# Where a mixer kernel stores its split weights, and which engine splits them before the first attention

## The chip, the cores and the metric

The kernel runs on one core of one Trainium2 chip. The metric is the device time of one execution in microseconds (us). Three executions of the kernel before gave 1756.65, 1754.84 and 1751.86 us, with a median of 1754.84 us.

## The reference, cut to what matters

One layer of a streaming encoder is computed for a prompt of 2048 rows and a sample of 32 rows, both 1024 wide and in float32.

```python
mod = c @ w_mod + b_mod                          # shift, scale, gate
h = rms_norm(x, g_pre) * (1 + scale) + shift
z = h @ w_in                                     # 1024 x 5632
a, b, z_conv, q, k, v, z_attn, g_conv, g_attn = split(z)
u = a * sigmoid(b)
y_conv = (silu(layer_norm(depthwise31(u) + dw_b)) * silu(z_conv)) @ w_conv_out
o = chunk_band_attention(q, k, v, rel_bias)      # 64-row chunks, own and 8 past chunks
y_attn = (o * silu(z_attn)) @ w_attn_out
merged = sigmoid(g_conv) * y_conv + sigmoid(g_attn) * y_attn
y = x + gate * rms_norm(merged @ w_o, g_post)
```

The new convolution rows, keys and values are returned as well.

## The kernel before, in words

The prompt is worked through in four blocks of 512 rows. Block 0 carries the 32 sample rows along, so its products have two halves of 272 columns, and the other blocks have one of 512.

Every product is done in two float32r parts. A weight W arrives in `raw` (512 KB), ScalarE copies its high part into `w`, and VectorE or GpSimd subtracts to get the low part. `w_parts` (L219) does this, and three matmuls follow for each pair of tiles. The weights come in one fixed order, the list `plan`. `weights` (L238) is called once for each of them. It splits the weight two places ahead (`w_parts(i + 2)`), loads the one four places ahead (`w_load(i + 4)`, two `raw` buffers), and stores the split one place ahead to DRAM (`w_keep(i + 1)`, 1 MB). Later uses load that 1 MB (`kept`) straight into one of three `w` buffers. `keep_at` (L207) says at which use a weight is stored. Before, the four weights of v are stored at their second use, in block 1, and all others at their first, in block 0 or, for some, behind it.

The stages of a block are these. The v projection comes first, then q and k of head pair 0. The attention follows, in units of one head and 256 query rows (or the sample), and between its parts `fill` lets the other projections run in the order of `FILL` (L54). In block 0 that order also holds eight parts `m0` to `m7` of the modulation gate (`mod_part`), four for each half, and `gate_row` finishes each half with one more matmul. After the attention come the gate projections (`C_GC`, `C_GA`, eight tiles each) with the attention's output product, then the convolution's output product, then w_o in two halves, with the a and b projections of the next block between them.

Before block 0 there is an opening stage. It computes shift and scale in four steps (`mod_load`, `mod_split`, `mod_mm`, `mod_vec`), normalises the rows, transposes them, and runs the v projection step by step.

The order on TensorE, VectorE, ScalarE and GpSimd is the order in which the program writes the instructions. It is steered by `Pace`, a clock kept by the program itself: `pace.pe` counts TensorE's time and `pace.dve` VectorE's, and `pace.start(gen, delay)` starts a side task when `pace.pe` has advanced by `delay`. The depthwise convolution's taps are such a side task (`pace.idle`). SP, which issues nearly all loads and stores, is not in that order: a planner places its DMAs, which is why `move_caches` (L594), written in block 1, is issued during block 0. ScalarE issues the stores of `w_keep`.

Which engine subtracts is decided in `w_parts`:

```python
on_v = pace.dense or pace.idle is None and pace.dve <= pace.pe + DV
(V if on_v else G).tensor_tensor(wl, raw, wh.bitcast(F32), op=OP.subtract)
```

`pace.dense` is set after the attention of block 0 and taken back after that of block 1.

Of the kernel before, what the change touches and what calls it, by code (L numbers as in the profile page):

```python
# [8 lines left out]
F32 = mybir.dt.float32  # L9
F32R = mybir.dt.float32r  # L10
I32 = mybir.dt.int32
AF = mybir.ActivationFunctionType
OP = mybir.AluOpType
# [3 lines left out]
P = 128  # L17
D = 1024
# [3 lines left out]
TB = 512  # L22
# [10 lines left out]
C_A, C_B, C_ZC, C_Q, C_K, C_V, C_ZA, C_GC, C_GA = (  # L33
    0, 512, 1024, 1536, 2048, 2560, 3072, 3584, 4608)
# [10 lines left out]
DV = -0.5  # L45
# [8 lines left out]
def FILL(b):  # L54

    part = dict(q=C_Q, k=C_K, a=C_A, b=C_B, z=C_ZA, c=C_ZC, m=C_MOD)
    order = "b0 a0 q1 m0 k1 m1 b1 m2 a1 m3 b2 q2 m4 k2 m5 a2 m6 z0 m7 b3 a3 z1 q3 k3 z2 z3 c0 c1 c2 c3" if b == 0 else \
        "q1 k1 z0 q2 k2 z1 q3 k3 z2 z3 c0 c1 c2 c3"
    return [(int(x[1]), part[x[0]]) for x in order.split()]


def dram(ap, off, dims):
    return bass.AP(tensor=ap.tensor, offset=ap.offset + off, ap=[list(d) for d in dims])
# [7 lines left out]
class Pace:  # L71


    def __init__(self):
        self.pe = 0.0
        self.dve = 0.0
        self.tasks = []
        self.idle = None
        self.lead = LEAD
        self.sinks = []  # L80
        self.dense = False

    def start(self, gen, delay=0.0):
        self.tasks.append([self.pe + delay, gen])
# [56 lines left out]
def mixer_kernel(ctx, tc, x_prompt, x_sample, c_prompt, c_sample, cache_conv, cache_k, cache_v,  # L141
# [4 lines left out]
    G = nc.gpsimd  # L146
    pace = Pace()
    V = Vec(nc, pace)

    def mm(out, lhsT, rhs, start, stop):  # L150
        n = 1
        for d in rhs.shape[1:]:
            n *= d
        pace.pe += (6 + n * 0.4063) / 1e3
        nc.tensor.matmul(out, lhsT=lhsT, rhs=rhs, start=start, stop=stop)  # L155
# [6 lines left out]
    wp = ctx.enter_context(tc.tile_pool(name="wp", bufs=2))  # L162
# [6 lines left out]
    def pp_tile(name):  # L169
        return pp.tile([P, 512], F32, tag="pp", name=name)  # L170
# [18 lines left out]
    for b in range(NB):  # L189
        plan += [w_wide("v", w_in, k, C_V) for k in range(0, KT, 2)]  # L190
        plan += [w_fill(n, c) for n, c in [(0, C_Q), (0, C_K)] + FILL(b)]
        for m in range(0, KT, 2):
            for i in range(2):
                plan += [w_cols(c + (m + i) * P) for c in (C_GC, C_GA)]
            plan.append(w_half("ao", w_attn_out, m))
        plan += [w_half("co", w_conv_out, m) for m in range(0, KT, 2)]
        plan += [w_wide("o", w_o, k, 0) for k in range(0, KT, 2)]
        if b < NB - 1:
            plan += [w_cols(c + ct * P) for ct in range(NCT) for c in (C_B, C_A)]
        plan += [w_wide("o", w_o, k, 512) for k in range(0, KT, 2)]  # L200

    uses = {}
    for i, entry in enumerate(plan):
        uses.setdefault(entry[0], []).append(i)
    keep_at = {key: at[1 if key[0] == "v" else 0] for key, at in uses.items()}  # L207
    again = {key for key, at in uses.items() if len(at) > 1}
    raws, halves, kept, used = {}, {}, {}, [0]

# [7 lines left out]
    def w_parts(i):  # L218

        if i < len(plan):  # L220
            key = plan[i][0]
            w = wp.tile([P, 2, 1024], F32R, tag="w", name="w", bufs=3)
            wh, wl = w[:, 0], w[:, 1]
            if i <= keep_at[key]:
                raw = raws.pop(i)
                act(wh, raw, AF.Copy)  # L226
                on_v = pace.dense or pace.idle is None and pace.dve <= pace.pe + DV
                (V if on_v else G).tensor_tensor(wl, raw, wh.bitcast(F32), op=OP.subtract)  # L228
            else:
                nc.sync.dma_start(w.bitcast(F32), kept[key])  # L230
            halves[i] = w
# [6 lines left out]
    def weights(key):  # L238
        i = used[0]
        assert plan[i][0] == key, (i, plan[i][0], key)  # L240
        used[0] += 1
        w_parts(i + 2)
        w_load(i + 4)
        w_keep(i + 1)
        w = halves.pop(i).rearrange("p h (k c) -> p h k c", c=plan[i][1])
        return w[:, 0], w[:, 1]
# [240 lines left out]
    def shape(b):  # L487
        yw = TB + (HIST + TS if b == 0 else 0)
        return TB + (TS if b == 0 else 0), yw, [(0, TB, 0)] + ([(USEP0, USEP0 + TS, TB)] if b == 0 else [])
# [74 lines left out]
    def mod_part(i):  # L564


        n, kp = i // 4, i % 4
        m4, bm, gr = aof[0:4, 3, 0:512], aof[0:2, 2, 0:512], aof[0:2, 1, 0:512]
        if kp == 0:
            nc.sync.dma_start(bm, dram(b_mod, 2 * D + n * 512, [[0, 2], [1, 512]]))  # L570
            nc.sync.dma_start(gr, dram(g_post, n * 512, [[0, 2], [1, 512]]))
        wh, wl = weights(("mod", 2 * kp, (4 + n) * 512))
        pm = pp_tile("pm")
        for kk in range(2):
            mm(pm[0:4], c4[:, 2 * kp + kk, :], wh[:, kk, :], kk == 0, False)
            mm(pm[0:4], c4[:, 2 * kp + kk, :], wl[:, kk, :], False, kk == 1)
            yield
        if kp == 0:
            act(m4, pm[0:4], AF.Copy)
        else:  # L580
            V.tensor_tensor(m4, pm[0:4], m4, op=OP.add)
        if kp == 3:
            pace.start(gate_row(n, m4, bm, gr), 1.5)

    def gate_row(n, m4, bm, gr):
        pg = pp_tile("pg")
        nc.tensor.matmul(pg[0:2], lhsT=sel, rhs=m4, start=True, stop=True)
        yield 1.5
        V.tensor_tensor(bm, pg[0:2], bm, op=OP.add)
        V.tensor_tensor(bm, bm, gr, op=OP.mult)  # L590
        nc.sync.dma_start(gp_d[:, n * 512:(n + 1) * 512], bm)
        gate_done.add(n)
        yield 0.0
# [7 lines left out]
    def spill_v(b, vcur):  # L601
        for t in range(4):
            nc.sync.dma_start(vs_d[b][:, t], vcur[:, t].bitcast(F32))
            yield 6.0
# [20 lines left out]
    with tc.tile_pool(name="init", bufs=1) as ini:  # L625
        mraw, mparts, m4 = {}, {}, {}
# [10 lines left out]
        def mod_split(c, start=0, end=4):  # L637
            mparts.setdefault(c, [])
            for i, raw in enumerate(mraw[c]):
                if i < start or i >= end:  # L640
                    continue
                wh, wl = [ini.tile([P, 4, 256], F32R, tag=n, name=n, bufs=4) for n in ("wmh", "wml")]
                act(wh, raw, AF.Copy)
                (G if i % 2 else V).tensor_tensor(wl, raw, wh.bitcast(F32), op=OP.subtract)
                mparts[c].append((wh, wl))

        pms = {}
# [42 lines left out]
        with tc.tile_pool(name="x0", bufs=5) as x0:  # L690
# [31 lines left out]
            c2 = vecs[:, 0:16].rearrange("p (a k) -> p k a", a=2)  # L722
# [7 lines left out]
            for t, (xt, m) in enumerate(xs0):  # L730
                if t % 2:
                    act(xt[0:m], xt[0:m], AF.Copy, scale=rr[0:m, t:t + 1])
                else:
                    V.tensor_scalar(xt[0:m], xt[0:m], rr[0:m, t:t + 1], None, op0=OP.mult)
            mod_mm(0, 0, 2)
            w_parts(0)
            pst = ps.tile([P, 512], F32, tag="T", name="pst", bufs=2)
            for ct in range(KT):
                transpose(pst[:, ct * TS:(ct + 1) * TS], xs0[4][0][0:TS, ct * P:(ct + 1) * P], ident[0:TS, 0:TS])
            xst = ini.tile([P, KT, TS], F32, name="xst")  # L740
            V.tensor_copy(xst, pst[:, 0:KT * TS].rearrange("p (k c) -> p k c", c=TS))
            pts = [h_turn(xs0, ct) for ct in range(2)]
            mod_split(1, 0, 2)
            mod_mm(0, 2)
            mod_vec(0)
            mod_split(1, 2, 4)
            lrow = aof.rearrange("p a c -> p (a c)")[0:H, 0:SKEW]

# [50 lines left out]


    pace.dve = pace.pe
    qls = []
    for b in range(NB):
        NT, YW, ypieces = shape(b)
# [4 lines left out]
        with tc.tile_pool(name="at", bufs=1) as at:  # L809
# [3 lines left out]
            vcur = at.tile([P, 4, H, P], F32R, name="vcur")  # L813
# [22 lines left out]
                    o = (nvs[0, 0, 512 - TS:512] if t == 4 else nvp[0, 0, t * P:(t + 1) * P])  # L836
                    nc.sync.dma_start(o.rearrange("t h d -> t (h d)"), vo[0:m, 0:512])
            if b < NB - 1:
                pace.start(spill_v(b, vcur), 30.0)

            if b < 2:

                qls.clear()
                for _ in range(2):
                    qls.append(wp.tile([P, 2, TB], F32R, tag="raw", name="ql0") if b else
                               at.tile([P, 2, NT], F32R, tag="ql", name="ql", bufs=2))
                    G.memset(qls[-1][64:128, 0].bitcast(F32), 0.0)
                    G.memset(qls[-1][0:64, 1].bitcast(F32), 0.0)


            att, cvs, ready = {}, {}, set()
# [95 lines left out]
            def z_proj(col, dst, key):  # L947
# [5 lines left out]
                def done():  # L953
# [4 lines left out]
            kind = {C_Q: q_proj, C_K: k_proj,  # L958
                    C_B: lambda n: b_proj(b, n), C_A: lambda n: a_proj(b, n, tmp),
                    C_MOD: mod_part,  # L960
                    C_ZA: lambda n: z_proj(C_ZA + n * P, aof[:, n], ("za", n)),
                    C_ZC: lambda n: z_proj(C_ZC + n * P, zcb[:, n], ("zc", n))}

            def side():
                for n, c in FILL(b):
                    yield from kind[c](n)
# [480 lines left out]
```

## Time and profile before

| | |
|---|---|
| median of three runs | 1754.84 us (1751.86 to 1756.65) |
| the profiled execution's own time | 1752.31 us |
| its span | 1750.5 us |
| TensorE busy | 1676.9 us, 96% of the span |
| VectorE, ScalarE, GpSimd busy | 1122.5, 633.5, 234.6 us |
| mean granted TensorE clock | 0.988 |

Durations are taken from this one execution. TensorE's busy time is modelled and includes the time in which it ran at half of its clock. A row of a timeline gives the start, the duration, the engine, the line, the operation, output <- input, and in brackets the engine's idle time before it with what ended that wait. L136 is the helper through which all VectorE instructions are written, L155 and L159 are those of matmuls and transposes.

### The profile page before, as it was taken

The page shows a single profiled execution, that of the slowest core. Times are in us where ns is not written, and L with a number is a line of the kernel's source. Part 1 is how long each engine was busy: PE and PEld are TensorE (multiplying, and loading weights), DVE is VectorE, ACT ScalarE, POOL GpSimd, SP SyncE. Part 2 cuts the span into 40 slices and gives each one's busy share as a digit, 9 for nine tenths or more (in the row PEclk, how much of TensorE's full clock was granted, in tenths as well). Part 3 has the DMA queues.
Part 4 walks back from the last instruction along what each step waited for, and adds up shares of the span by engine and source line. Part 5 has one row for each costly group of instructions (what it writes and reads, how often), then busy time and mean ns, then how long its engine had stood idle before and what let it go on. Part 6 is the DMA issues. An engine that isn't in the chain of part 4 may idle for free.

```text
span 1750.5 us, 23607 instructions
## 1 busy us (share of the span) xinstructions
PE 1676.9 (96%) x9221; PEld 1428.5 (82%) x9221; DVE 1122.5 (64%) x2030; ACT 633.5 (36%) x1218; POOL 234.6 (13%) x174
## 2 busy tenths in 40 slices
PE   6978889999999999999999999999999999999997
PEld 4767779999878788888788888888888888888886
DVE  6457878796737867674544967774543967665423
ACT  6544534424721255522331045531330045531211
POOL 5423332101310000001120000001120000001120
PEclk9998999999999999999999999999999999999999
DMA  8786455776675774465455674465555674455553
GB/s 271 238 286 227 164 200 207 263 277 224 235 261 207 269 276 167 148 226 190 172 217 182 236 272 179 153 221 190 181 216 188 220 262 150 148 181 195 189 192 144
DMA packets 132326, 368.61 MB, mean 211 GB/s; under 512 B 9326, under 2 KB 75050, under 8 KB 101975
## 3 DMA queue, kind: packets, MB, share of 16 engines
q1 hardware_dynamic: 123575, 304.19, 50.4%
q10 hardware_dynamic: 8640, 62.92, 8.8%
q8 instruction: 73, 1.20, 0.3%
q14 instruction: 38, 0.31, 0.1%
HBM read 280.41 MB, written 91.77 MB: 213 GB/s over the span
## 4 chain that ended last, share of the span: by engine, by line
PE 73%; DVE 4%; ACT 2%; DMA 1%; issue 1%; POOL 0%; POOLq 0%; ACTq 0%; DVEq 0%
PE pj L155 41%; PE py L155 9%; PE pv L155 4%; PE op L155 3%; PE sps L155 3%; PE pt L159 3%; PE oT L155 3%; PE oS L155 3%; PE vS L155 2%; PE vT L155 2%; PE oP L155 1%; DMA raw<-in_w_in_dram 1%; DVE pre L136 1%; DMA raw<-in_w_attn_out_dram 1%; PE pxt L159 0%
## 5 line engine op out<-in xcount | busy, mean ns | idle before, releaser
L155 PE MATMUL pj<-hh,w 128*128 128x512 f32 (+1 forms) x4800 | 975.9, 357 | 12.7 <-DVE kk L136 5.4
L155 PEld LDWEIGHTS pj<-hh,w 128*128 128x128 f32 x4800 | 782.6, 190 | 134.7 <-ACT kk L863 4.9
L136 DVE SCALAR_TENSOR_TENSOR y<-u,dww,y 128x512 f32<-128x512 f32 (+1 forms) x480 | 345.9, 781 | 0.5
L1084 ACT ACTIVATE sp<-sp,mn 128x640 f32<-128x640 f32 (+5 forms) x136 | 103.6, 762 | 133.9 <-DVE mn L136 133.9
L1119 ACT ACTIVATE pth<-pt 128x256 fp32r<-128x256 f32 (+4 forms) x184 | 91.8, 500 | 135.1 <-PE pt L159 123.7
L136 DVE TENSOR_TENSOR ptl<-pt,pth 128x256 fp32r<-128x256 f32 (+4 forms) x184 | 104.0, 565 | 28.1 <-ACT pth L1119 26.7
L228 POOL TENSOR_TENSOR w<-raw,w 128x1024 fp32r<-128x1024 f32 x37 | 92.2, 2497 | 177.3 <-ACT w L226 147.7
L136 DVE CUSTOM_DVE_ANT_0 sp<-sps,bias 128x640 f32<-128x640 f32 (+4 forms) x128 | 94.1, 735 | 26.5 <-PE sps L155 25.5
L155 PE MATMUL py<-ah,w 128*128 128x512 f32 (+1 forms) x480 | 96.0, 356 | 6.9 <-DVE t L136 4.8
L226 ACT ACTIVATE w<-raw 128x1024 fp32r<-128x1024 f32 x72 | 75.7, 1052 | 70.5 <-PE py L155 17.0
L155 PEld LDWEIGHTS py<-ah,w 128*128 128x128 f32 x480 | 79.8, 192 | 20.5 <-DVE t L136 5.2
L159 PE MATMUL pt<-ident,sp 128*128 128x128 f32 (+1 forms) x600 | 95.2, 274 | 0.0
L155 PE MATMUL py<-cohi,w 128*128 128x512 f32 (+1 forms) x320 | 90.1, 357 | 1.6 <-DVE mg L136 1.6
L532 POOL TENSOR_TENSOR u<-y 128x512 f32<-128x512 f32 (+1 forms) x4 | 5.3, 1324 | 641.5 <-DVE y L136 591.0
L136 DVE TENSOR_SCALAR sp<-sp,ll 128x640 f32<-128x640 f32 (+5 forms) x136 | 84.5, 621 | 4.8
L155 PE MATMUL sps<-kk,qh 128*128 128x320 f32 (+1 forms) x224 | 70.3, 321 | 9.1 <-DVE mn L136 8.3
L159 PEld LDWEIGHTS pt<-ident,sp 128*128 128x128 f32 (+1 forms) x600 | 69.6, 141 | 3.6 <-issue 1.3
L1347 POOL TENSOR_TENSOR mg<-mg,t 128x512 f32<-128x512 f32 (+1 forms) x32 | 46.4, 1451 | 172.2 <-issue 118.8
L155 PE MATMUL sps<-kk,ql 128*128 128x320 f32 (+1 forms) x224 | 68.5, 313 | 0.0
L1311 ACT ACTIVATE t<-pj 128x512 f32<-128x512 f32 (+1 forms) x40 | 20.7, 517 | 127.6 <-PE pj L155 127.4
L136 DVE SCALAR_TENSOR_TENSOR t<-t,py 128x512 f32<-128x512 f32 (+1 forms) x40 | 23.2, 584 | 67.1 <-PE py L155 67.0
L155 PEld LDWEIGHTS py<-cohi,w 128*128 128x128 f32 x320 | 56.7, 188 | 9.8 <-DVE mg L136 2.3
(255 smaller groups left out, 2250.4 us busy)
## 6 DMA issues: line engine op xcount, KB each, us to landing
w<-kept SPq DMA_DIRECT2D x176, 1024.0 KB, 4.8
kept<-w ACTq DMA_DIRECT2D x60, 1024.0 KB, 4.7
raw<-in_w_in_dram SPq DMA_DIRECT2D x48, 512.0 KB, 4.9
bias<-bias_d SPq DMA_DIRECT2D x32, 320.0 KB, 5.5
xt<-in_x_prompt_dram SPq DMA_DIRECT2D x16, 512.0 KB
wm<-in_w_mod_dram SPq DMA_DIRECT2D x16, 512.0 KB, 7.4
xr<-in_x_prompt_dram SPq DMA_DIRECT2D x16, 512.0 KB, 4.6
vs_d<-vcur SPq DMA_DIRECT2D x12, 512.0 KB
```

The source lines that it names most:

```text
L136: return fn(out, *a, **k)
L155: nc.tensor.matmul(out, lhsT=lhsT, rhs=rhs, start=start, stop=stop)
L159: nc.tensor.transpose(out, in_, idn)
L226: act(wh, raw, AF.Copy)
L228: (V if on_v else G).tensor_tensor(wl, raw, wh.bitcast(F32), op=OP.subtract)
L532: G.tensor_tensor(s2[:, 0:YW], Y[2][:, 0:YW], Y[3][:, 0:YW], op=OP.add)
L1084: self.ex[i] = lambda: act(sp[0:m, 0:nk], sp[0:m, 0:nk], AF.Exp, bias=mn[0:m], scale=-1.0, accum_out=ll[0:m])
L1119: act(self.ph[0:r, f0:f1], pt[0:r, o:o + f1 - f0], AF.Copy)
L1311: pace.run(proj(C_GC + m * P, b, lambda o, c0, c1: act(t1[:, c0:c1], o, AF.Tanh, scale=0.5)))
L1347: G.tensor_tensor(mg, mg, t2, op=OP.add)
```

## The change

- `keep_at`: the weights of q and k of head pair 0, and the gate weights of tiles 2 to 7 (12 of 16), are stored at their second use, so in block 1, and not in block 0. In block 1 these 14 weights are therefore loaded and split once more. The gate weights' second subtraction is always VectorE's.
- `pace.dense` begins as True and is taken back ahead of block 0, so all weight subtractions of the opening stage are VectorE's; those of `mod_split` are VectorE's too.
- In block 0's `FILL` the parts m0 to m7 come later by one to three projections.
- `gate_row` starts 4.0 in place of 1.5 after its half's last part.
- In block 0 `spill_v`, which stores v for block 1 (four stores of 512 KB), starts 100 in place of 30 after the v projection.
- The two `ql` buffers are taken anew and cleared in blocks 2 and 3 as well, since the `raw` buffers that they lie in are now used by block 1's gate weights.

```diff
-    order = "b0 a0 q1 m0 k1 m1 b1 m2 a1 m3 b2 q2 m4 k2 m5 a2 m6 z0 m7 b3 a3 z1 q3 k3 z2 z3 c0 c1 c2 c3" if b == 0 else \
+    order = "b0 a0 q1 k1 b1 m0 a1 m1 b2 m2 q2 m3 k2 m4 a2 m5 z0 m6 b3 m7 a3 z1 q3 k3 z2 z3 c0 c1 c2 c3" if b == 0 else \
...
-        self.dense = False
+        self.dense = True
...
+    def gate(key):
+        return key[0] == "in" and key[1] >= C_GC
+
+    def twice(key):
+        if gate(key):
+            return (key[1] - C_GC) % D >= 2 * P
+        return key[0] == "v" or key in (("in", C_Q), ("in", C_K))
+
...
-    keep_at = {key: at[1 if key[0] == "v" else 0] for key, at in uses.items()}
+    keep_at = {key: at[1 if twice(key) else 0] for key, at in uses.items()}
...
-                on_v = pace.dense or pace.idle is None and pace.dve <= pace.pe + DV
+                on_v = pace.dense or gate(key) and i > uses[key][0] or pace.idle is None and pace.dve <= pace.pe + DV
...
-            pace.start(gate_row(n, m4, bm, gr), 1.5)
+            pace.start(gate_row(n, m4, bm, gr), 4.0)
...
-                (G if i % 2 else V).tensor_tensor(wl, raw, wh.bitcast(F32), op=OP.subtract)
+                V.tensor_tensor(wl, raw, wh.bitcast(F32), op=OP.subtract)
...
     pace.dve = pace.pe
+    pace.dense = False
...
-                pace.start(spill_v(b, vcur), 30.0)
-
-            if b < 2:
-
-                qls.clear()
...
+                pace.start(spill_v(b, vcur), 100.0 if b == 0 else 30.0)
+
+            qls.clear()
```

## Rows read from the trace of the kernel before

**Rows 1.** Windows: stretch, its length, busy time of each engine, granted clock, DMA share, GB/s.

```profile
core 0: us, PE busy (x) PEld busy (x) DVE busy (x) ACT busy (x) POOL busy (x), PEclk, DMA share, GB/s
20.00:75.00 55.00, 50.60 (x293) 37.52 (x292) 34.51 (x51) 33.49 (x50) 34.53 (x25) 0.97 0.74 229
80.00:100.00 20.00, 13.21 (x103) 12.44 (x101) 7.28 (x16) 10.41 (x22) 6.31 (x3) 0.96 1.00 323
80.00:330.00 250.00, 218.03 (x1600) 197.97 (x1599) 182.93 (x385) 117.95 (x273) 81.34 (x36) 0.95 0.64 216
330.00:460.00 130.00, 122.89 (x961) 121.66 (x960) 103.40 (x148) 52.29 (x90) 19.43 (x14) 0.99 0.76 272
600.00:620.00 20.00, 20.00 (x89) 16.38 (x88) 12.61 (x20) 4.55 (x8) 1.74 (x2) 1.00 1.02 376
763.00:802.00 39.00, 39.00 (x170) 31.56 (x169) 38.28 (x59) 3.60 (x6) 0.00 (x0) 1.00 0.69 259
802.00:862.00 60.00, 57.63 (x249) 46.42 (x248) 29.21 (x48) 20.87 (x34) 11.54 (x9) 1.00 0.48 175
```

**Rows 2.** Timeline of TensorE in the opening stage.

```profile
29.51 0.28 PE L155 MATMUL pm<-wml,c 128*4 128x256 f32 x1 [1.15 <-POOL wml L644]
...
48.34 1.05 PE L676 MATMUL pc<-sel,m 4*128 4x2 f32 x8 [2.47 <-DVE m L136]
...
50.17 2.60 PE L155 MATMUL vS<-w,hh 128*128 128x512 f32 x6
...
63.85 1.64 PE L155 MATMUL vS<-w,hh 128*128 128x512 f32 x6
```

**Rows 3.** Timeline of VectorE in the opening stage.

```profile
26.00 1.22 DVE L136 TENSOR_TENSOR wml<-wm,wmh 128x1024 fp32r<-128x1024 f32 x1
27.35 2.65 DVE L136 TENSOR_TENSOR hh<-hf,hh 128x512 fp32r<-128x512 f32 x1
...
30.02 0.68 DVE L136 TENSOR_TENSOR hh<-hf,hh 128x512 fp32r<-128x512 f32 x1
...
31.79 6.14 DVE L136 TENSOR_TENSOR wml<-wm,wmh 128x1024 fp32r<-128x1024 f32 x2 [0.35 <-ACT wmh L643]
...
44.80 2.57 DVE L136 TENSOR_SCALAR aof<-aof,rv 8x512 f32<-8x512 f32 x1 [1.00 <-POOL aof L766]
```

**Rows 4.** Timeline of GpSimd in the opening stage.

```profile
40.16 2.84 POOL L228 TENSOR_TENSOR w<-raw,w 128x1024 fp32r<-128x1024 f32 x1
...
44.73 2.36 POOL L644 TENSOR_TENSOR wml<-wm,wmh 128x1024 fp32r<-128x1024 f32 x1
```

**Rows 5.** Timeline of TensorE at the first attention units of block 0.

```profile
101.27 0.69 PE L155 MATMUL sps<-kk,qh 128*128 128x384 f32 x1 [6.74 <-DVE mn L136]
...
102.08 2.92 PE L155 MATMUL pj<-hh,w 128*128 128x272 f32 x12
...
105.43 1.67 PE L155 MATMUL pj<-hh,w 128*128 128x272 f32 x12
```

**Rows 6.** Timeline of ScalarE there (ACTq is its DMA issue).

```profile
80.91 0.35 ACTq L236 DMA_DIRECT2D kept<-w  x1
...
97.32 1.06 ACT L226 ACTIVATE w<-raw 128x1024 fp32r<-128x1024 f32 x1 [6.86 <-DMA raw<-in_w_in_dram]
```

**Rows 7.** Timeline of SP's DMA issues there.

```profile
81.02 1.47 SPq L603 DMA_DIRECT2D vs_d<-vcur  x3
...
85.14 1.31 SPq L216 DMA_DIRECT2D raw<-in_w_in_dram  x1
...
95.36 0.64 SPq L596 DMA_DIRECT2D out_dram<-in_cache_k_dram  x1
```

**Rows 8.** Timeline of TensorE at the gate's second half.

```profile
231.67 1.86 PE L587 MATMUL pg<-aof,sel 4*2 4x512 f32 x2 [3.72 <-DVE aof L136]
```

**Rows 9.** Timeline of TensorE in block 1's v and q projections.

```profile
597.97 1.42 PE L155 MATMUL vS<-w,hh 128*128 128x512 f32 x5 [2.39 <-DVE w L136]
...
608.94 11.38 PE L155 MATMUL pj<-hh,w 128*128 128x512 f32 x49
```

**Rows 10.** The page's DMA issues: count, KB each, median us from issue to landing.

```profile
raw<-in_w_in_dram SPq DMA_DIRECT2D x48, 512.0 KB, 4.9
```

More of the change, by code (lines that the diff above doesn't have):

```diff
@@ L838, in mixer_kernel @@
             if b < NB - 1:
-                pace.start(spill_v(b, vcur), 30.0)
-            if b < 2:
-                qls.clear()
[L844 to L848, printed above, removed]
+                pace.start(spill_v(b, vcur), 100.0 if b == 0 else 30.0)
+            qls.clear()
+            for _ in range(2):
+                qls.append(wp.tile([P, 2, TB], F32R, tag="raw", name="ql0") if b else
+                           at.tile([P, 2, NT], F32R, tag="ql", name="ql", bufs=2))
+                G.memset(qls[-1][64:128, 0].bitcast(F32), 0.0)
+                G.memset(qls[-1][0:64, 1].bitcast(F32), 0.0)
             att, cvs, ready = {}, {}, set()
```

## The prediction, made blind

> **What bounds the kernel now.** I read the windows first, then TensorE's waits, then the timelines around the longest of them. TensorE sets the end, busy for 96% of the span: an edit is worth only what it takes from TensorE's waits or adds to them. Of its 1750.5 - 1676.9 = 73.6 idle us, 43.5 lie in three stretches of block 0. From 80 to 330 us TensorE is idle 250 - 218.0 = 32 us, and the granted clock is 0.95 on average, which is some 0.05 x 218 = 11 us more; from 20 to 75 us it is idle 55 - 50.6 = 4.4 us, and from 330 to 460 us 130 - 122.9 = 7.1 [rows 1]. In the first two of them the change has about 47 us to work on, and most of that belongs to waits that it does not touch (VectorE late with scores and with k's parts).
>
> The reader is to see three things in the rows. First, in the opening stage VectorE and GpSimd get in each other's way: while GpSimd subtracts, VectorE's instructions with the same shape take 2.65 us in place of 0.68, or 6.14 us for two in place of 2 x 1.22 [rows 3], and a tiny one of 2.57 us ends just behind the GpSimd subtraction that began with it and took 2.36 [rows 3, 4]. Second, the longest wait of block 0, 6.74 us at 94.5 us [rows 5], is ScalarE standing 6.86 us at a weight's copy because the weight has not landed [rows 6]; exponentials, normalisation and scores queue behind that copy. The weight was issued at 85.1 us, behind three stores of v at 81.0 [rows 7] and a store of a split weight at 80.9 [rows 6], while the DMA engines were full (share 1.00, 323 GB/s, [rows 1]). Third, a stall costs more than its length: after it twelve matmuls of 272 columns took 2.92 us, and 3 us later 1.67 us [rows 5].
>
> **The opening stage.** Eleven subtractions go from GpSimd to VectorE: six of `mod_split`, and those of the weights 0 to 4, as only the sixth was VectorE's already. VectorE gains 11 x 1.22 = 13.4 us of work and loses the blocked time of the rows shown: 2.65 - 0.68 = 2.0, 6.14 - 2.44 = 3.7, and about 2 of the 2.57, so 7.7; net at most 5.7 us, and VectorE is busy 34.5 of 55 us there [rows 1, 3], so there is room. The results also come sooner: 1.22 us against 2.36 to 2.84 [rows 3, 4], without GpSimd's queue, in which the subtraction at 40.16 held back SP's next weight. What TensorE can win are its wait of 1.15 us for GpSimd and that of 2.47 us for a copy which stood on VectorE behind the blocked 2.57 us, with the half-clock matmuls after it: six took 2.60 us against 1.64, and the next group lost some 0.6 more [rows 2]. That is 5.2 us at most. The least is nothing: VectorE has four subtractions in a row ahead of each `mod_vec`, and that one could be late instead. I follow the order by hand and find the four shift and scale steps at about the same time as now or 1 us later early on, and the third step free of the 2.47 us wait. I take 3.5.
>
> **The crowd at 80 to 100 us.** The store of k's weight at 80.91 leaves (1 MB, 3.2 us at 323 GB/s); that of q's, earlier, had room around it. The stores of v are 4 x 0.52 MB, 6.5 us, if they really leave this stretch. They are written 30 in the program's clock after the v projection, so near 104 us, and were issued at 81.0; the copy of the cache is written in block 1 and was issued at 95.4 [rows 7]. SP's planner thus takes what is ready when it has a gap, and 100 in place of 30 lets other ready DMAs go first but need not hold the stores back. I expect them some 10 us later, ahead of the cache copies. Then the weight at 85.1 is not behind them and the wait of 6.74 goes, but the next weight meets them. Low end: only the 1 MB goes, 3.2 us. High end: the whole wait and the slow matmuls after it, 6.74 + 2.92 - 1.67 = 8.0. I take 5.5. The modulation parts, 0.5 MB each for little TensorE time, move out of this stretch too, and k's and b's weights with their stores come in: no net.
>
> The Trainium skill, in DMA: Bandwidth & Descriptors (Queues, rings and completion order), says that each DMA engine takes turns between the queues that have work, packet by packet. No row here shows the turns. By it, and with three v stores gone from SP's queue, the weight would have only an equal amount of ScalarE's stores beside it, and 5.5 would be about 6.5; the sum keeps 5.5.
>
> **The gate row.** TensorE waits 3.72 us for VectorE before the second half's last matmul [rows 8]. Starting it 2.5 later in the program's clock puts other matmuls ahead, so up to 3.72 and some 1.2 of slow matmuls (as in rows 5) can go. But m7 moves behind b3, where another VectorE queue stands, and the new order of `FILL` can put some other sink in the way. From 0 to 4.9; I take 2.5. The order itself I cost at 0, with 4 us either way: it decides which matmul meets VectorE late, and nothing in the rows says in which sense.
>
> **Block 0's gates.** Twelve stores of 1 MB leave 360 to 420 us. DMA share in this stage is 0.76 [rows 1] and its waits are mostly for VectorE and ScalarE: 0.
>
> **Block 1's price.** The weights of q0 and k0 are loaded as raw and split again. q0's load needs the buffer of the third v weight, whose subtraction ended at 598 us, since TensorE waited for it [rows 9]. With the median landing of 4.9 us [rows 10], ScalarE's 1.06 [rows 6] and VectorE's 1.22 [rows 3] it is ready at 605.2, ahead of 608.9, where TensorE begins q0 [rows 9]. The DMA engines are full here, 1.02 and 376 GB/s [rows 1], and with the 12.2 us of the weight in rows 6 and 7 it is ready at 612.5, 3.6 us late. From 0 to 3.6; I take 1, as the load is half of the 1 MB that it replaces.
>
> The 12 gate weights add 12 x 1.22 = 14.6 us to VectorE and 12 x 1.06 = 12.7 us to ScalarE between 770 and 862 us. VectorE is full with taps until 802 (38.3 of 39 us) and then half idle (29.2 of 60) [rows 1]. Four or five of them fall before 802, so the convolution ends 5 to 6 us later; behind it there is room. Block 0's stage of the same form carries all these subtractions and is idle those 7.1 us, block 1's 60 - 57.6 = 2.4 [rows 1]: that bounds the cost by 4.7 us. Least 0; I take 1. The extra stores have room (share 0.48 to 0.69). Clearing `ql` in blocks 2 and 3 is eight small writes on a GpSimd that has next to nothing to do: 0, and if it were late, q's sink would wait some 2 us for each block.
>
> **Sum.** 3.5 + 5.5 + 2.5 - 1 - 1 = 9.5 us gained. From the profiled execution's 1752.3 that gives 1742.8; the median shown is 2.5 us higher, and from it one gets 1745.3. A result is a median too, so I forecast 1745.
>
> **Rivals.** *The planner leaves v's stores where they are* (what the change says it does is then half done), and the waits only move. For it: the issue times of rows 7. Against: priority does change. Then 3.5 + 3.2 + 0 - 2 = 4.7: 1750.
>
> *All of it comes through*: 5.2 + 8.0 + 4.9 - 1 = 17: 1738, and a lucky order makes it 1734. For it: each of the three waits has its own cause that is named and taken away. Against: bytes only move, and the DMA engines are full beyond 100 us too.
>
> *Block 1's VectorE becomes the bound* (slower). The 14.6 us come while VectorE has no idle time; sinks of the output products and the convolution's tail stand behind them, and TensorE waits for both. For it: VectorE's 38.3 of 39 us. Against: the half idle stretch after 802. Price: the 4.7 us above, and with q0's 3.6 late, 8.3; it decides the sign where block 0 gives back less than that, so with only the 3.2 of the crowd: 1754.8 - 3.2 + 8.3 = 1760.
>
> **Chances.** Forecast 0.47 (1739 to 1749), all of it 0.16, stores of v stay 0.24, block 1's price 0.13. What a measurement of this kernel can tell from no change is about 0.3%, 5.3 us, so the borders are 1749.6 and 1760.1. Faster: the first two and a quarter of the third, 0.69. Same: the rest of the third and some of the fourth, 0.24. Slower: 0.07. The range of 8 in 10 reaches from the middle of the second case to beyond the third: 1734 to 1755; the forecast's own is 1739 to 1749.
>
> **What would show it.** Right: no GpSimd subtraction before 75 us, VectorE's 128x512 subtractions all near 0.68 us there, the first attention starting 2 to 5 us earlier; ScalarE not standing at a weight around 90 us; TensorE idle 80 to 330 us down from 32 to some 22 us; the gate's row without a wait. Wrong: v's stores again at the start of the crowd; a new wait of over 3 us on a weight between 90 and 130 us; TensorE idle at the start of q0 in block 1, or more than 4 us more idle time between 755 and 875 us.

## The result, and the profile after

The changed kernel takes 1742.67 us (four runs, 1741.4 to 1744.33), the kernel before in the same comparison 1755.42 (four runs, 1751.86 to 1756.65): ratio 0.993, 95% interval 0.9914 to 0.9946. It is faster by 0.7%, some 12 us. The profiled execution took 1743.5 us with a span of 1741.4, so the two traces differ by 8.8 us (1752.31 before): the one of before is a quick run among its kind. Below, traces say where time went, and ratios say how much. One of the ten executions of the kernel e1 below, at a granted clock of 0.654, took 2345.47 us and is left out of its ratio.

The windows of the kernel after, columns as in [rows 1]:

```profile
20.00:75.00 55.00, 52.59 (x319) 39.28 (x318) 35.44 (x66) 34.97 (x54) 4.99 (x17) 1.00 0.83 245
80.00:100.00 20.00, 15.87 (x120) 14.75 (x120) 10.02 (x24) 10.69 (x24) 5.93 (x3) 1.00 0.91 310
80.00:330.00 250.00, 223.26 (x1660) 203.65 (x1660) 188.22 (x394) 119.41 (x274) 82.12 (x36) 0.96 0.63 220
330.00:460.00 130.00, 121.73 (x950) 120.27 (x949) 101.21 (x148) 54.73 (x93) 21.01 (x16) 0.99 0.47 160
755.00:875.00 120.00, 120.00 (x527) 97.34 (x526) 92.50 (x133) 43.68 (x65) 16.33 (x11) 1.00 0.71 254
```

TensorE is idle 2.4 us in the opening stage (4.4 before), 4.1 us at 80 to 100 (6.8 before) and 26.7 us at 80 to 330 (32), a window in which some 8 us more of the program now lie. GpSimd's busy time in the opening stage falls from 34.5 to 5.0 us. VectorE's, with eleven subtractions more, goes from 34.5 to 35.4: what it gained in work it lost in blocked time.

The timelines of the opening stage after, TensorE and then VectorE, against [rows 2, 3]:

```profile
39.79 0.28 PE L155 MATMUL pm<-wmh,c 128*4 128x256 f32 x1 [1.07 <-DVE Gm L136]
...
46.77 1.05 PE L684 MATMUL pc<-sel,m 4*128 4x2 f32 x8
48.60 1.63 PE L155 MATMUL vS<-w,hh 128*128 128x512 f32 x6
```

```profile
28.95 0.68 DVE L136 TENSOR_TENSOR hh<-hf,hh 128x512 fp32r<-128x512 f32 x1
...
33.27 4.61 DVE L136 TENSOR_TENSOR wml<-wm,wmh 128x1024 fp32r<-128x1024 f32 x4
...
44.65 0.48 DVE L136 TENSOR_SCALAR aof<-aof,rv 8x512 f32<-8x512 f32 x1 [1.01 <-POOL aof L774]
```

Four subtractions in a row take 4.61 us where two took 6.14, the tiny one takes 0.48 us in place of 2.57, and `pc` no longer waits 2.47 us. A new wait of 1.07 us stands at 39.79, for a `Gm` that now comes behind those four subtractions and one more. GpSimd's first subtraction is now this one:

```profile
78.83 2.39 POOL L236 TENSOR_TENSOR w<-raw,w 128x1024 fp32r<-128x1024 f32 x1 [4.41 <-PE pj L155]
```

The crowd after: TensorE, ScalarE (ACTq is its DMA issue), SP, against [rows 5 to 7]:

```profile
94.83 0.45 PE L155 MATMUL sps<-kk,qh 128*128 128x384 f32 x1 [3.32 <-DVE mn L136]
...
95.29 1.67 PE L155 MATMUL pj<-hh,w 128*128 128x272 f32 x12
...
98.77 0.39 PE L155 MATMUL sa<-kk,qh 128*32 128x512 f32 x1
```

```profile
82.19 0.34 ACTq L244 DMA_DIRECT2D kept<-w  x1
...
90.87 1.06 ACT L234 ACTIVATE w<-raw 128x1024 fp32r<-128x1024 f32 x1 [3.45 <-DMA raw<-in_w_in_dram]
```

```profile
74.99 0.68 SPq L611 DMA_DIRECT2D vs_d<-vcur  x1
...
81.81 0.54 SPq L611 DMA_DIRECT2D vs_d<-vcur  x1
...
82.87 0.90 SPq L224 DMA_DIRECT2D raw<-in_w_in_dram  x1
83.86 2.90 SPq L611 DMA_DIRECT2D vs_d<-vcur  x2
```

The wait of 6.74 us is 3.32, and the twelve matmuls behind it are not at half clock any more (1.67 us, not 2.92). But ScalarE still stands 3.45 us at a weight, and v's stores, which the change writes later, are issued at 75 to 87 us, no later than before. The gate row waits too, now for its first half:

```profile
182.63 1.86 PE L595 MATMUL pg<-aof,sel 4*2 4x512 f32 x2 [2.51 <-DVE ql L136]
```

In block 1 there is one new wait. Its cause is three pieces of the chain that ended last in the kernel after, and TensorE's row:

```profile
588.79 6.91 DMA raw<-in_w_in_dram
595.86 8.63 DMA kept<-w
604.54 8.84 DMA w<-kept
```

```profile
613.51 2.34 PE L155 MATMUL pj<-hh,w 128*128 128x512 f32 x9 [2.57 <-DMA w<-kept]
```

ScalarE stands at q0's raw weight until 595.77. The store of the last v weight is behind that copy in ScalarE's order, so it leaves only at 595.86. It holds the `w` buffer that q1's weight needs, whose load is issued at 604.54 and lands 2.6 us after TensorE is ready for it.

### The profile page after: what moved, and what is told of

Same layout as the page of the kernel before. It is cut to its first block, busy times and chain, and to the rows that moved or that the text cites. A ratio compares the mean times of both kernels' runs of the same rounds, so it can differ in the third digit from the quotient of the medians.

```text
span 1741.4 us, 23645 instructions
## 1 busy us (share of the span) xinstructions
PE 1674.9 (96%) x9221; PEld 1425.8 (82%) x9221; DVE 1135.9 (65%) x2055; ACT 646.5 (37%) x1232; POOL 210.3 (12%) x171
## 4 chain that ended last, share of the span: by engine, by line
PE 63%; DMA 2%; DVE 1%; ACT 0%; POOL 0%; issue 0%; POOLq 0%; DVEq 0%; ACTq 0%; SPq 0%
PE pj L155 35%; PE py L155 8%; PE pv L155 4%; PE sps L155 3%; PE pt L159 3%; PE op L155 3%; PE oT L155 2%; PE oS L155 2%; PE vS L155 1%; PE vT L155 1%; PE oP L155 1%; DMA w<-kept 1%; DMA kept<-w 0%; PE pxt L159 0%; DMA raw<-in_w_in_dram 0%; DVE pre L136 0%
## 5 line engine op out<-in xcount | busy, mean ns | idle before, releaser
L234 ACT ACTIVATE w<-raw 128x1024 fp32r<-128x1024 f32 x86 | 90.3, 1053 | 99.2 <-DMA raw<-in_w_in_dram 30.5
L236 POOL TENSOR_TENSOR w<-raw,w 128x1024 fp32r<-128x1024 f32 x32 | 81.3, 2547 | 150.7 <-ACT w L234 114.2
L136 DVE TENSOR_TENSOR w<-raw,w 128x1024 fp32r<-128x1024 f32 x54 | 69.5, 1288 | 41.5 <-ACT w L234 40.9
L136 DVE TENSOR_SCALAR sp<-sp,ll 128x640 f32<-128x640 f32 (+5 forms) x136 | 78.6, 578 | 4.8
```

What stands on the lines that cost most here:

```text
L136: return fn(out, *a, **k)
```

## The experiments

The table has every kernel by the stages of its trace on TensorE, in us: to the first matmul of q; from there to the first `sa` (the crowd); to the first `py<-ah` of block 0; to its first `py<-cohi`; to q of block 1; to `py<-ah` there; to `py<-cohi` there. What follows takes 877 to 878 us in each. The ratio is to the kernel before in the same comparison.

| kernel | to q | crowd | to ah | to cohi | to q, 1 | to ah, 1 | to cohi, 1 | median us | ratio |
|---|---|---|---|---|---|---|---|---|---|
| before | 74.4 | 32.6 | 243.5 | 107.6 | 151.0 | 171.5 | 93.0 | 1755.42 | 1 |
| after | 71.8 | 26.9 | 241.5 | 108.6 | 150.9 | 174.3 | 90.5 | 1742.67 | 0.9930 |
| e1 opening alone (trace: second run) | 71.4 | 31.2 | 244.5 | 107.5 | 150.9 | 172.0 | 94.5 | 1747.96 | 0.9964 |
| e8 opening, row | 72.1 | 32.8 | 237.2 | 107.7 | 152.5 | 171.5 | 92.9 | 1744.66 | 0.9944 |
| e7 after, old order | 71.5 | 30.2 | 234.3 | 106.2 | 151.0 | 175.9 | 90.5 | 1739.24 | 0.9923 |
| e6 after, row 1.5 | 71.6 | 30.1 | 237.7 | 106.3 | 150.9 | 176.5 | 90.5 | 1741.06 | 0.9928 |
| e5 after, v at 30 (one run) | 71.6 | 28.3 | 238.0 | 107.7 | 152.5 | 173.1 | 90.5 | 1740.47 | |
| e2 after, q0/k0 first | 71.3 | 28.2 | 243.3 | 107.8 | 152.4 | 171.5 | 90.6 | 1744.63 | 0.9945 |
| e3 after, gates first | 72.2 | 28.5 | 238.6 | 108.1 | 152.5 | 172.9 | 90.6 | 1741.92 | 0.9935 |
| e4 after, store ahead | 71.9 | 28.7 | 247.9 | 111.8 | 152.5 | 177.8 | 90.5 | 1760.59 | 1.0040 |
| e9 e7, v by ScalarE | 71.8 | 25.8 | 235.1 | 107.5 | 152.5 | 172.9 | 90.5 | 1736.03 | 0.9900 |
| e10 e9, caches too | 71.8 | 25.6 | 235.8 | 107.6 | 152.5 | 172.8 | 90.5 | 1734.88 | 0.9892 |
| e11 e10, gates first | 71.7 | 25.7 | 235.2 | 105.9 | 151.0 | 176.7 | 90.6 | 1735.49 | 0.9889 |

Kernels that do not differ in a stage still differ there by 1 to 3 us: the crowd takes 26.9 us in the changed kernel, 28.5 in e3 and 30.1 in e6, whose edits lie behind it. So one trace's difference under 3 us in a stage carries nothing by itself. The half widths of the ratios' intervals are 0.0012 to 0.0035, so a difference of two of them is sure to about 0.002, 3.5 us, and with e3 or e11 to 0.003 to 0.004.

The column "to q, 1" has two values, near 151.0 and 152.5, and the reason shows in each trace. TensorE waits 2.39 us for VectorE in block 1's v projection in every kernel. Behind that wait it runs at full clock in some traces (granted 1.00 from 588.8 to 592 us in the changed kernel) and at half in others (0.50 from 590.5 to 593.5 us in e2). The changed kernel, then e2:

```profile
588.82 1.43 PE L155 MATMUL vS<-w,hh 128*128 128x512 f32 x5 [2.38 <-DVE w L136]
```

```profile
590.53 2.50 PE L155 MATMUL vS<-w,hh 128*128 128x512 f32 x5 [2.39 <-DVE w L136]
```

Where TensorE came to q later by this, it waits less for q1's weight: 1.0 to 1.3 us in e3, e5, e9 and e10, against 2.6 to 3.4 in the changed kernel, e6, e7 and e11. So "to q, 1" and "to ah, 1" are to be read together.

**The opening stage alone.**

```diff
# e1, against before
-        self.dense = False
+        self.dense = True
-                (G if i % 2 else V).tensor_tensor(wl, raw, wh.bitcast(F32), op=OP.subtract)
+                V.tensor_tensor(wl, raw, wh.bitcast(F32), op=OP.subtract)
     pace.dve = pace.pe
+    pace.dense = False
```

> The kernel before with one part of the change: every subtraction of the opening stage on VectorE (w_mod's halves and the first weights), the switch back before block 0. Nothing of the stores, the gate row or the filler's order. Theory (the parts add up, the crowd at 80 to 100 us moves with its start): the first query projection starts at 71.8 us as in the changed kernel (74.4 before), the wait of the second score unit for the query's VectorE copies stays at 6.7 +- 1 us, first sa at 104.4, end 2.5 us earlier: 1752.9 us, ratio 0.9986. Rival (the crowd is ended by transfers that the opening doesn't bring forward): first sa again at 106.9, the wait grows to 9.2 us, time 1755.4, ratio 1.000.

Measured: 1747.96 us, ratio 0.9964 (0.9952 to 0.9976). That is 6.3 us, more than either theory had. It was run once more for its trace:

> The kernel of the first run once more, for its trace (the opening stage on VectorE alone): it took 1748.0 us, 6 us less than before, where the two theories had 2.5 and 0. Theory now: the 2.5 us at the first query projection and a crowd that is lighter by itself, because its first transfers start earlier against the same later ones: first sa at 101 +- 1 us (before 106.9, changed kernel 98.8), and the rest as before, end at 1745. Rival: the gain beyond 2.5 us is not at the crowd but behind it (the gate row's wait, block 0's gate stage): first sa at 104.4, and the first py<-ah of block 0, 350.4 before, at 344 to 345.

This run took 1750.72 us, above the other nine of the kernel (up to 1750.46), so its trace shows little of the gain beyond the opening stage. q begins at 71.4 and first `sa` comes at 102.6, 4.3 us earlier than before: 0.6 us above the theory's range, and below the rival's 104.4. The long wait did not go, it moved to k's matmuls. TensorE, then ScalarE, of that run:

```profile
91.76 3.55 PE L155 MATMUL pj<-hh,w 128*128 128x272 f32 x15 [6.96 <-DVE kk L136]
```

```profile
89.88 0.39 ACT L863 ACTIVATE kk<-pj 64x272 fp32r<-64x272 f32 x1 [6.46 <-DMA out_dram<-vo]
```

ScalarE stands 6.46 us, as it stood 6.86 [rows 6], at another transfer of the same crowd. So the opening stage makes the crowd begin earlier and does not make it lighter (31.2 and, in e8, 32.8 us against 32.6).

**The stores of q0 and k0.**

```diff
# e2, against after
-        return key[0] == "v" or key in (("in", C_Q), ("in", C_K))
+        return key[0] == "v"
```

> The changed kernel, with the split weights of q0 and k0 stored again at their first use, in block 0, and read from there in block 1. Theory: these two stores of 1 MB are what the crowd at 80 to 100 us lost, so they bring most of it back: the wait ahead of the second score unit goes from 3.3 to 6 to 8 us and first sa from 98.8 to 102 to 104; in block 1 the 2.57 us wait for q1's kept weight at 613.5 goes, because ScalarE no longer stands 14 us at q0's raw weight ahead of the store of the last v weight. Net +1 to +2.5 us: 1744 to 1745. Rival (the crowd became lighter by the earlier opening and the filler's order, not by the two stores): first sa stays at 98.8 +- 0.7, and only block 1's gain is left: 1740.1.

Measured: 1744.63 us, ratio 0.9945 (0.9926 to 0.9965), not separated from the changed kernel. The time is the theory's, but the crowd is close to the rival: it takes 28.2 us, 1.2 more, and the wait ahead of the second score unit is 0.31 us. A wait stands earlier in its place, at q's matmuls:

```profile
84.47 3.17 PE L155 MATMUL pj<-hh,w 128*128 128x272 f32 x15 [3.90 <-DVE ql L136]
```

In block 1 the stage with the new wait is back at 171.5 us from 174.3, without that wait. The stage ahead of it has the slow matmuls, and the two together take 323.9 us against 325.2, 1.3 less. So with the new filler's order the two stores are worth nothing in the crowd that stands out of its scatter, and their price in block 1 is 1.3 to 2.8 us.

**The stores of the gates.**

```diff
# e3, against after
-            return (key[1] - C_GC) % D >= 2 * P
+            return False
```

> The changed kernel, with the twelve gate weights stored at their first use again (no gate is read raw a second time). Theory: the gate stage of block 0 (from its first matmul to the first of the convolution's output, 316.1 to 448.9) becomes the 1.0 us or so longer that it is in the kernel changed... that is, it gets back the 131.7 us of the kernel before, from 132.7 (-1.0), and that of block 1 (751.9 to 864.6, 112.7) becomes 115.3 again (+2.5), with a wait near its end: 1744.2 us. Rival (the gate stage of block 1 gained from its earlier weights' order, not from these stores): block 1 stays at 112.7, block 0 gains 1.0: 1741.7.

Measured: 1741.92 us, ratio 0.9935 (0.991 to 0.996): the rival. Block 1's stage stays at 90.6, so the 2.5 us that it is shorter after the change do not come from these stores. Block 0's (108.1 against 108.6) tells nothing.

**The store put ahead of the next split.**

```diff
# e4, against after
+        w_keep(i + 1)
         w_parts(i + 2)
         w_load(i + 4)
-        w_keep(i + 1)
```

> The changed kernel, with the store of a kept weight put ahead of the split of the next one in ScalarE's order (w_keep(i + 1) before w_parts(i + 2)). Theory: at the start of block 1's query the store of the last v weight waits behind ScalarE's 14 us stand at q0's raw weight, holds its buffer, and so delays the load of q1's kept weight; with the store ahead of it the wait of 2.57 us at 613.5 falls below 0.5 us and the end comes 2 to 2.6 us earlier: 1740.3. Rival: ScalarE now stands at stores that wait for the subtraction of the low half (2.4 us on GpSimd), its conversions and evictions come later, and TensorE waits for them in the attention of block 0 and in the gate stages: 1744 to 1748.

Measured: 1760.59 us, ratio 1.004 (1.0026 to 1.0054): slower than the kernel before. The wait for q1's kept weight is gone, as expected, but others took its place, most of them in block 0. In its gate stage, ScalarE and then TensorE:

```profile
343.98 1.06 ACT L234 ACTIVATE w<-raw 128x1024 fp32r<-128x1024 f32 x1 [8.74 <-DMA raw<-in_w_attn_out_dram]
...
354.72 1.06 ACT L234 ACTIVATE w<-raw 128x1024 fp32r<-128x1024 f32 x1 [5.65 <-DMA raw<-in_w_in_dram]
```

```profile
359.35 3.09 PE L155 MATMUL py<-ah,w 128*128 128x272 f32 x12 [6.21 <-DVE t L136]
```

ScalarE stands at raw weights that come late, not at subtractions as the rival had it. Why they come late when the store is written ahead of the split was not tried.

**The delay of v's stores.**

```diff
# e5, against after
-                pace.start(spill_v(b, vcur), 100.0 if b == 0 else 30.0)
+                pace.start(spill_v(b, vcur), 30.0)
```

> The changed kernel with the delay of block 0's stores of v back at 30 in place of 100. Theory (SP's order is made by the planner, which put these stores at 75 to 87 us with 100 as with 30): the stores stand at 75 to 87 us again, every milestone of the trace within 0.7 us of the changed kernel's up to first sa, end within 2 us of 1741.4. Rival (the delay moves other transfers of SP): first sa comes 1.5 us or more later, the end 2 us or more.

Measured: 1740.47 us in one run. SP's rows in that kernel:

```profile
76.29 2.59 SPq L611 DMA_DIRECT2D vs_d<-vcur  x3
80.38 0.98 SPq L611 DMA_DIRECT2D vs_d<-vcur  x1
```

With 30 the stores are issued at 76.3 to 81.4, with 100 at 75.0 to 86.8. The number does not keep them out of the crowd. First `sa` comes 1.1 us later and the end 3 us earlier, outside what either theory had, but one run does not tell 2 us from nothing.

**The gate row, and the filler's order.**

```diff
# e6, against after
-            pace.start(gate_row(n, m4, bm, gr), 4.0)
+            pace.start(gate_row(n, m4, bm, gr), 1.5)
# e7, against after
-    order = "b0 a0 q1 k1 b1 m0 a1 m1 b2 m2 q2 m3 k2 m4 a2 m5 z0 m6 b3 m7 a3 z1 q3 k3 z2 z3 c0 c1 c2 c3" ...
+    order = "b0 a0 q1 m0 k1 m1 b1 m2 a1 m3 b2 q2 m4 k2 m5 a2 m6 z0 m7 b3 a3 z1 q3 k3 z2 z3 c0 c1 c2 c3" ...
```

> The changed kernel with the gate row's delay back at 1.5 in place of 4.0. Theory: both of its rows wait for the modulation's halves again as the one at 231.67 did before (about 4.9 us there; 2.5 us at 182.63 is left in the changed kernel), so the stage from first sa to the first py<-ah of block 0, 241.5 us in the changed kernel and 243.5 before, takes 2 to 2.5 us more: 1744.9 us. Rival (what the row waits is taken from waits behind it, or the filler's order has moved the halves far enough ahead): within 0.7 us, 1742.7.

> The changed kernel with block 0's filler in its old order (m0 third, k1 and a1 later). Theory (the order counts for little, as forecast): within 1 us, 1742 to 1743.7. Rival (what the whole has beyond the opening stage alone, 5.2 us, and that the stores of q0, k0 and the gates leave unexplained, is this order): 1745 to 1747, and the loss stands between first sa and the first py<-ah of block 0.

Measured: e6 1741.06 us, ratio 0.9928 (0.9911 to 0.9944), and e7 1739.24, ratio 0.9923 (0.9906 to 0.9939). Neither edit of the change is missed when it is taken back alone. In e6 the gate row does not wait: in the new order the short delay suits it better. In e7 it does not wait either: in the old order the long one does. With the old order the crowd takes 30.2 us against 26.9, but e6 has 30.1 with the new one. Up to 100 us TensorE and SP work in the same order in e6 as in the changed kernel; SP only issues the weight at 84.85 us and not at 82.87, and the wait is the longer for it. SP and TensorE in e6:

```profile
84.85 1.20 SPq L224 DMA_DIRECT2D raw<-in_w_in_dram  x1
```

```profile
96.31 0.69 PE L155 MATMUL sps<-kk,qh 128*128 128x384 f32 x1 [4.64 <-DVE mn L136]
```

So what the order is worth in the crowd is not shown. In the stage behind it the orders stand apart: with the delay of 4.0, the old one takes 234.3 to 237.2 us (e7 to e11), the new one 238.0 to 243.3 (the changed kernel, e2, e3, e5; e4 left aside). By the whole runs they are not told apart: 0.0007 in the ratio, with an uncertainty of 0.0023.

**The row without the stores.**

```diff
# e8, against before: e1's edits, and
-            pace.start(gate_row(n, m4, bm, gr), 1.5)
+            pace.start(gate_row(n, m4, bm, gr), 4.0)
```

> The kernel before with the opening stage on VectorE (as in the first run) and the gate row's delay at 4.0; the stores and the filler's order as before. Theory: in that order the row's wait of 3.7 us at 231.67 goes with the longer delay, as it did in the changed kernel with the old order, so the time is 3 to 4 us under the opening stage alone (1748.0): 1744.5 us, and what is then left to 1739.2 (old order, all else changed) is the stores', 5 us. Rival (the stores are what moved the row's halves ahead, the delay alone does nothing): 1748, with the row's wait of 3.7 us still there.

Measured: 1744.66 us, ratio 0.9944 (0.993 to 0.9959): the theory. TensorE's rows of the gate in this kernel, against [rows 8], neither with a wait:

```profile
170.13 1.02 PE L587 MATMUL pg<-aof,sel 4*2 4x512 f32 x2
...
228.88 1.01 PE L587 MATMUL pg<-aof,sel 4*2 4x512 f32 x2
```

In the old order the delay brings the third stage from 243.5 (244.5 in e1) to 237.2 us, where only 3.7 us of wait and about 0.8 us of slow matmul stood at the row. The rest of that stage's difference is not put down to anything.

**v's stores really later, and the caches' copies.** The change says that block 0's stores come later. On ScalarE's queue, whose order is the program's, they do:

```diff
# e9, against e7
-            nc.sync.dma_start(vs_d[b][:, t], vcur[:, t].bitcast(F32))
+            (nc.sync if b else nc.scalar).dma_start(vs_d[b][:, t], vcur[:, t].bitcast(F32))
# e10, against e9: move_caches, both copies
-        nc.sync.dma_start(...)
+        nc.scalar.dma_start(...)
```

> The changed kernel with the old order of the filler, and block 0's four stores of v (2 MB) issued from ScalarE's queue, whose order is the program's, in place of SP's, where the planner puts them at 75 to 87 us whatever their delay: so they really come later, some 100 us on. Theory (the raw weights of the crowd land late because these stores share the transport with them): the wait ahead of the second score unit, 5.2 us with the old order, falls to 2.5 us or less, first sa from 101.7 to 98 to 99, end 2.5 to 3 us earlier: 1736.5 us. Rival (SP's planner moves the two cache copies, 2 MB, into the same gap, or the chain is ScalarE's and VectorE's own): first sa stays at 101 to 102 and the time at 1739.2.

> The kernel of the run before (old order, stores of v on ScalarE's queue), with the two copies of the caches (1 MB each) on ScalarE's queue as well, where they come after block 1's first key projection, in place of 91 to 113 us. Theory (the crowd): if the planner has put the copies into the gap that the stores of v left, this takes them out too: first sa at 97 to 98, end 1 to 2 us under the run before. Rival: the copies, which then run beside block 1's loads of kept weights from 616 us, make a wait there of 2 us or more, and the time is no better than without them.

Measured: e9 1736.03 us, ratio 0.99 (0.9884 to 0.9917), e10 1734.88, ratio 0.9892 (0.9877 to 0.9906). First `sa` comes at 97.6 and 97.4 us. e10 is below the changed kernel by 0.38%, with an uncertainty of 0.22%; it is not told apart from e9, and its copies make no wait in block 1 beyond the 1.0 us at q1 (1.2 in e9). So e9's theory has its numbers, but for 0.4 us at the first `sa`. Its mechanism is not quite that one. SP, ScalarE and TensorE in e7, and then in e10:

```profile
76.67 0.59 SPq L611 DMA_DIRECT2D vs_d<-vcur  x1
...
83.57 0.54 SPq L611 DMA_DIRECT2D vs_d<-vcur  x1
...
85.44 1.23 SPq L224 DMA_DIRECT2D raw<-in_w_in_dram  x1
86.76 1.54 SPq L611 DMA_DIRECT2D vs_d<-vcur  x2
```

```profile
92.42 1.06 ACT L234 ACTIVATE w<-raw 128x1024 fp32r<-128x1024 f32 x1 [5.32 <-DMA raw<-in_w_in_dram]
```

```profile
96.37 0.69 PE L155 MATMUL sps<-kk,qh 128*128 128x384 f32 x1 [5.18 <-DVE mn L136]
```

```profile
82.54 0.40 SPq L224 DMA_DIRECT2D raw<-in_w_in_dram  x1
```

```profile
89.50 1.06 ACT L234 ACTIVATE w<-raw 128x1024 fp32r<-128x1024 f32 x1 [2.11 <-DMA raw<-in_w_in_dram]
...
208.57 0.34 ACTq L611 DMA_DIRECT2D vs_d<-vcur  x1
```

```profile
93.47 0.44 PE L155 MATMUL sps<-kk,qh 128*128 128x384 f32 x1 [1.98 <-DVE mn L136]
```

From issue to ScalarE's copy the weight takes 7.0 us in both, with v's stores around it and without them. What goes in this pair is 2.9 us of the time at which SP issues it, and the wait ahead of the second score unit falls by 3.2 us, from 5.18 to 1.98. Over all traces with q0's and k0's stores put off, ScalarE begins this copy at 89.5 to 89.7 us without v's stores on SP (e9 to e11) and at 90.6 to 92.4 with them. But the issue times overlap (81.2 to 83.4 against 81.5 to 85.4), and so do the ways from issue to copy (6.1 to 8.5 against 7.0 to 9.1). So which part of the way the stores lengthen is not settled.

In the kernel before the same way took 12.2 us, with two stores of 1 MB on ScalarE's queue and not one, and with three of v's stores just ahead of the weight on its own queue. ScalarE's two stores alone do not make it so long. In e2 they are issued at nearly the same times, and the copy starts 5.2 us after the weight's issue. ScalarE, then SP in e2:

```profile
81.36 0.35 ACTq L244 DMA_DIRECT2D kept<-w  x1
...
86.87 0.33 ACTq L244 DMA_DIRECT2D kept<-w  x1
...
91.12 1.04 ACT L234 ACTIVATE w<-raw 128x1024 fp32r<-128x1024 f32 x1
```

```profile
85.95 0.57 SPq L224 DMA_DIRECT2D raw<-in_w_in_dram  x1
```

The Trainium skill, in DMA: Bandwidth & Descriptors (Queues, rings and completion order), lets each DMA engine take turns between queues, packet by packet. No row shows the turns, and these times do not bear them out: beside two stores on the other queue the weight took 12.2 us in one kernel and at most 5.2 in another.

**All that helped, together.**

```diff
# e11, against e10: e3's edit
```

> The kernel of the run before (old order of the filler, stores of v and copies of the caches on ScalarE's queue), with the twelve gate weights stored at their first use again: the fastest parts together. Theory (keeping the gates raw once more is worth nothing: with or without it the stage from the first py<-ah to the first py<-cohi of block 1 takes 90.5 us, and block 0's from 0.5 to 1 us less with the stores early): 1733 to 1735 us, ratio to before 0.988 to 0.990. Rival (the gates' stores do matter once the crowd is light): 1736 to 1738, with a wait in block 0's or block 1's gate stage that the run before has not.

Measured: 1735.49 us, ratio 0.9889 (0.9854 to 0.9924): level with e10. As far as these runs tell, the gates may be stored early or late.

## Why the prediction was right, and where it was not

The time was forecast at 1745 us and came at 1742.67; faster was the likeliest case. The traces differ by 8.8 us where the sum had 9.5. Going by ratios along e1, e8, e7 and the changed kernel, with 1754 us as 1, the opening stage gave 6.3 us (0.0036), the row's delay 3.5 (0.0020), the stores with the rest of the edits 3.7 (0.0021), and the new order took 1.2 (0.0007): 12.3 in all. Of these only the first is clearly outside its uncertainty.

**The opening stage** (3.5): the mechanism was right. No subtraction is on GpSimd before 78.8 us, VectorE's rows have their unblocked lengths, the 2.47 us wait is gone, and the risk named, a `mod_vec` late behind four subtractions, cost 1.07 us. The trace has 2.5 us at q. The runs of the part alone have 6.3, above the 5.2 that was its bound, and where the rest arises is not shown: in the one trace of it, q begins 3.0 us earlier than before, the first `sa` 4.3 and the end 1.6.

**The crowd** (5.5): the number was right in the changed kernel's trace, 5.6 us from q to first `sa`, and that was luck: e3 and e6, whose edits lie behind this stretch, gain 4.1 and 2.5 there. The step failed that explained it. It expected v's stores some 10 us later, so that the weight would not be behind them. They were at 75 to 87 us as ever, which is the first rival's mechanism, and its 3.2 us lie in the same span. ScalarE stood at a weight at 90.87, and TensorE is idle 26.7 us from 80 to 330, not some 22. What shortened the crowd is not put down to one edit: with the two stores taken back it takes 28.2 us (e2), with the order taken back 30.2 (e7), and both lie at or inside what kernels with neither taken back show, 26.9 to 30.1. Once v's stores did move (e9), the wait fell to 2.25 us from 5.18. Against e7 the weight was issued 4.2 us earlier there, and its way to ScalarE's copy was longer, 8.5 us and not 7.0.

**The row** (2.5) and **the order** (0): together 2.0 us between first `sa` and `py<-ah`. Both terms look mis-sized, with opposite signs. The delay was worth 3.5 us by the runs in the old order, just outside its uncertainty; the new order takes some 1 to 9 us more in this stage, and by the runs 1.2, which is not told from nothing. The row's wait was not removed: 2.51 us stand at the other half.

**Block 0's gates** (0): 1.0 us in the trace, within what equal stages scatter. Their sign was not settled.

**Block 1's price**: q0's weights (1) cost 1.3 to 2.8 us, but by another path. q0 itself was on time (599.80, after 9.1 us gained), and the delay went through ScalarE's stand into a store, from the store into a buffer and from there to q1's load. The working followed the raw weight and stopped there; it left out what is queued behind ScalarE's copy. It is within the range that was named, 0 to 3.6, and e11's 3.4 us at the same place shows its upper end. The gates (1) cost nothing: TensorE is busy 120 of 120 us at 755 to 875. The wait of 2.37 us that went there in block 1 is of another kind. VectorE and GpSimd in the kernel before:

```profile
842.69 1.22 DVE L136 SCALAR_TENSOR_TENSOR rt<-rr 128x8 f32<-128x8 f32 x1
843.94 1.22 DVE L136 TENSOR_TENSOR rt<-rt,ss 128x8 f32<-128x8 f32 x1
845.20 1.23 DVE L136 SCALAR_TENSOR_TENSOR rr<-rt,rr 128x8 f32<-128x8 f32 x1
846.45 0.17 DVE L136 TENSOR_TENSOR rt<-rr 128x8 f32<-128x8 f32 x1
```

```profile
841.34 5.06 POOL L560 TENSOR_TENSOR y<-y,u 128x512 f32<-128x512 f32 x4 [17.10 <-DVE ss L136]
```

Small operations of 0.17 us took 1.22 each beside GpSimd's four additions, and TensorE then waited 2.37 us for VectorE. Kernels before, e1 and e8 have this wait, all others have not. Which edit moved it was not settled: with any one of five taken back (e2, e3, e5, e6, e7) it stays away.

## What to carry to other kernels

A delay written in the program moves only what the program orders. Where a planner places an engine's DMAs, look at the issue times, and use a queue whose order is written if a transfer must come later: that was worth some 3 us here (e9 against e7: 4.4 us in the crowd, 0.0023 in the ratio with an uncertainty of as much, so not clear of nothing), and the number in the source nothing that showed. Before a stage's gain is put down to an edit, look at kernels that have the same instructions there: here three of them spread over 3.2 us. Cost a weight by what stands behind the engine that waits for it, down to the buffers that a store behind it holds. And take single edits back one by one: a change that wins 0.7% held one edit that gave about half of it, and others of which none is missed when it alone is taken back.

## What the runs showed of the hardware

Stores that stood behind a 512 KB weight on its own queue did not lengthen its way from issue to use: 7.0 us with two of them just behind it (e7) and without (e10). What made the same way 12.2 us in the kernel before is open. The same 2.39 us wait of TensorE was followed by matmuls at full clock in six traces and at half clock in seven, which cost those 1.5 us. And GpSimd's hold on VectorE reaches small operations as well: 0.17 us became 1.22, the length of one GpSimd addition (5.06 us for four). The Trainium skill, in SBUF — State Buffer (SBUF: two separate sides), has this as a lock that is held for a whole instruction, and the rows agree.
